# The first embedding's gate in seven block products, and all late weights in pools on one side

## The chip, the core and the metric

The kernel runs on one core of a Trainium2 chip. The metric is the device time of one execution in microseconds. Three runs of the kernel before took 3415.33, 3416.30 and 3417.81; the median is 3416.3. The engines are PE (matrix products, into PSUM), DVE (vector), ACT (scalar functions and copies), POOL (a second vector engine) and SP, which issues the DMAs. Each works through its own instructions in order, and semaphores tie them together.

## What is computed

The reference is a two-layer encoder over 2048 + 256 tokens of width 1024, in float32. What the change touches comes after the first layer's attention and after the second layer's mixer:

```python
h = h + y                                                   # y: attention's output projection
gate = jax.nn.sigmoid(rms_norm(h, norm_ple[0]) @ w_ple_gate[0])
h = h + gate * (p[0] @ w_ple_proj[0])                       # first embedding
y = mixer_c(rms_norm(h, norm_mix[1]), w_in_c, w_grp_c, scale_c, w_out_c)
h = h + y                                                   # y ends with @ w_out_c
gate = jax.nn.sigmoid(rms_norm(h, norm_ple[1]) @ w_ple_gate[1])
h = h + gate * (p[1] @ w_ple_proj[1])                       # second embedding
```

## The kernel before

Every product of two float32 matrices is made of three matmuls of the type fp32r: both operands are split in a high and a low part, and high x high, high x low and low x high are summed in PSUM (`mm3`, L176). In the trace such a triple reads `wh,ah`, `wl,ah`, `wh,al`: the first name is the operand that streams through (`wh`, `wl`: parts of the weights), the second the one that stands in the array (`ah`, `al`: parts of the activations). In the mixer the weights stand and the activations stream.

The program runs in stages: the first projections; attention A beside the second half of the projections; attention B beside "fill" work (output projection, embedding projections, folding of the mixer's weights, all by `drive`, which mixes a main generator and a fill generator by costs); the rest of the fill; then, from about 2370 us in the profile, the part that the change rewrites:

- The **gate of the first embedding** takes 18 tiles of 128 tokens. For each, `norm_rows` (L182) makes the normalised rows `xn` (ACT for the squares, POOL for the scale), `quarter` (L980) turns four blocks by PE transposes into `pt`, `part` (L973) splits them into `ah` (ACT) and `al` (DVE), and `gate_half` (L950) makes 512 columns of the product in 8 chunks of 128 channels, that is 24 matmuls, then the sigmoid (ACT), the product with the embedding `pp` and the sum with the residual `xr` (DVE). Its weights `WG0` stand in the pools `ple0a` and `ple0b`, opened from the right side of SBUF.
- In the same loop `halves_sums` (L1029) makes sums of weights for the two later stages: loads of four quarter blocks, four differences on POOL, four stores (`to_d`, `tg_d`).
- The **mixer** works on blocks of 256 tokens and four groups `g`. A group has two products of 48 matmuls x 256 columns: `pg` with `WG[g]`, `pz` with `WU[g]`. Its weights stand in four pools `wc0` to `wc3`, opened from the left side; `load_c` (L1011) fills them.
- The **mixer's output projection and the second embedding's gate** (`Pair`, L1120, and the loop at L1343) use Strassen's scheme in Winograd's form on pairs of token tiles: two by two blocks, seven products of 4 chunks x 3 = 12 matmuls instead of eight. `Pair.prepare` makes the sums of activations for the next pair, `Pair.use` adds up the products. The seven weight blocks (`BLK`) take over the mixer's pools (`HOME`); `block_w` (L1091) loads and splits one. While the last pair of the output projection runs, each block is replaced by that of the gate.

The order of instructions on each engine is set when the program is built: a scheduler places them by simulated times, within what the pools' and tiles' waits allow. Weights and stagings come through `slot()`, four buffers of 128x512 (`wst`). All loads and stores go through SP's queue.

A tile's place in SBUF is fixed in the built program. There the tiles `ah`, `al` and the gate's `wh`, `wl` (pools from the right) start 32 bytes beside a multiple of 64; the mixer's and the seven products' `wh`, `wl` (pools from the left) start at multiples of 64, as do all operands of the first projections.

Of the kernel before, what the change touches and what calls it, by code (L numbers as in the profile page):

```python
# [11 lines left out]
F32 = mybir.dt.float32  # L12
# [21 lines left out]
WG_A = 6  # L34
# [5 lines left out]
def trunk_kernel(ctx: ExitStack, tc: tile.TileContext, ins, outs):  # L40
# [37 lines left out]
    t_d = [[dscratch(f"t{n}{i}_d", [512, 512]) for i in range(4)] for n in "og"]  # L78
# [675 lines left out]

    ahead = {}
# [25 lines left out]
    def proj_out(k0):  # L781
# [22 lines left out]
        for i, tq in enumerate(todo):  # L804
# [5 lines left out]
            for a in (0, 512):  # L810
                xr, nx = nx, before(i, a + 512)
                ps = fill_ps()
                for c in range(4):
                    mm3(ps, (yh[:, c], yl[:, c]), W[a // 512][c], c == 0, c == 3)
                    if c == 1:
                        yield 1.3 * (OUTK if k0 else 1.0)
                ve.tensor_tensor(out=xr, in0=ps, in1=xr, op=ALU.add)
                sy.dma_start(h_d[tq : tq + P, a : a + 512], xr)
                if a == 0:
                    y = fetched(i + 1)  # L820
                    if k0 == 0 and i == len(todo) - 1:
                        fill_w(("ple", 0))
                yield 1.3 * (OUTK if k0 else 1.0)

# [125 lines left out]
    def gate_half(pw, layer, W, n_, tq, a, pg, sg, xr, dst):  # L950

        cols = slice(a, a + 512)
        if a == 0:
            sg.append(pw.tile([P, D], F32, tag="pp", name="pp", bufs=1))
            sy.dma_start(sg[1], pp_d[layer][tq : tq + P])
        for c in range(KC):
            mm3(pg, [x[:, c % 4] for x in n_[c // 4]], (W[c][0][:, cols], W[c][1][:, cols]), c == 0, c == KC - 1)
        ac.activation(sg[0][:, cols], pg, AF.Sigmoid)
        ve.tensor_tensor(out=sg[0][:, cols], in0=sg[1][:, cols], in1=sg[0][:, cols], op=ALU.mult)
        ve.tensor_tensor(out=xr[:, cols], in0=xr[:, cols], in1=sg[0][:, cols], op=ALU.add)  # L960
        if a:
            sy.dma_start(dst, xr)

    xr_ = [(0, NXR)]

    def loaded(tq):
        o, n = xr_[0]
        xr_[0] = (o + 1) % n, n
        xr = (late if o == NXR else work).tile([P, D], F32, tag=f"xr{o}", name="xr", bufs=1)
# [17 lines left out]
    def turned(xn):  # L987
        return [part(quarter(xn, k), ve) for k in range(2)]

    ple0 = [ExitStack(), ExitStack()]  # L990
    wpg = ins["w_ple_gate"][0]
    pw = ple0[0].enter_context(tc.tile_pool(name="ple0a", bufs=1, side="right", reuse_waits="tile"))
    WG0 = load_w(pw, wpg[: WG_A * P], WG_A * P, [(0, D)], "wg", gple[0][:, :WG_A])
    for _ in fill:
        pass
    keep.close()
    sS_.close()
    xr = loaded(0), loaded(P)
    pw = ple0[1].enter_context(tc.tile_pool(name="ple0b", bufs=1, side="right", reuse_waits="tile"))
    WG0 += load_w(pw, wpg[WG_A * P :], D - WG_A * P, [(0, D)], "wg", gple[0][:, WG_A:])  # L1000
    n_ = turned(norm_rows(work, xr[0]))

    wc = ins["w_in_c"][0]
    WU, WG = [], []
    wp = []

    def pair_w(g, c):

        return [wp[g].tile([P, 512], F32R, tag=f"{x}{c}", name=f"w{x}", bufs=1) for x in "hl"]

    def load_c(g):  # L1011

        wp.append(ctx.enter_context(tc.tile_pool(name=f"wc{g}", bufs=1, reuse_waits="tile")))
        both = [pair_w(g, c) for c in range(KC)]
        for to, src, o in ((WU, m_d, g * 256), (WG, wc, D + g * 256)):
            i = 0 if to is WU else 256
            got = [[t[:, i : i + 256] for t in b] for b in both]
            for c in range(0, KC, 2):
                st = slot().rearrange("p (k w) -> p k w", k=2)
                sy.dma_start(st, src[c * P : (c + 2) * P, o : o + 256].rearrange("(k p) w -> p k w", p=P))  # L1020
                for k in range(2):
                    split_w(st[:, k], *got[c + k], gmix[1][:, c + k : c + k + 1])
            to.append(got)

    first_x = []

    w_tail = ins["w_out_c"][0], ins["w_ple_gate"][1]

    def halves_sums(pool, n, c):  # L1029

        q = []
        for i in range(4):
            k, a = divmod(i, 2)
            b = pool.tile([P, 512], F32, tag=f"q{i}", name="q", bufs=2)
            sy.dma_start(b, w_tail[n][k * 512 + c * P : k * 512 + c * P + P, a * 512 : a * 512 + 512])
            if n:
                ac.activation(b, b, AF.Copy, scale=gple[1][:, k * 4 + c : k * 4 + c + 1])
            q.append(b)
        b11, b12, b21, b22 = q
        for i, (out, x, y) in enumerate(((b11, b12, b11), (b12, b22, b12), (b22, b22, b11), (b21, b21, b22))):  # L1040
            po.tensor_tensor(out=out, in0=x, in1=y, op=ALU.subtract)
            sy.dma_start(t_d[n][(0, 2, 1, 3)[i]][c * P : c * P + P], out)

    for tq in range(0, T, P):
        more = tq + P < T
        sg = [pw.tile([P, D], F32, tag="sg", name="sg")]
        if more:
            xn = norm_rows(work, xr[1])
        else:
            first_x.append(norm_rows(work, loaded(0)))  # L1050
        gate_half(pw, 0, WG0, n_, tq, 0, po_(), sg, xr[0], h_d[tq : tq + P])
        if more:
            n2 = turned(xn)
        else:
            first_x.append(norm_rows(work, loaded(P)))
        gate_half(pw, 0, WG0, n_, tq, 512, pf_(), sg, xr[0], h_d[tq : tq + P])
        if more:
            xr, n_ = (xr[1], loaded(tq + 2 * P) if tq + 2 * P < T else None), n2
        if tq == 4 * P:
            load_c(0)  # L1060
        if tq // P - 6 in range(8):
            halves_sums(pw, *divmod(tq // P - 6, 4))

    def turned2(xn):

        got = []
        for j in range(4):
            pt = pt_()
            for c in range(2):
                for i in range(2):  # L1070
                    pe.transpose(pt[:, (c * 2 + i) * P : (c * 2 + i + 1) * P], xn[i][:, (j * 2 + c) * P : (j * 2 + c + 1) * P], ident)
            got.append([x.rearrange("p c t -> p (c t)").rearrange("p (c t) -> p c t", t=NB) for x in part(pt, ve)])
        return got

    x0 = turned2(first_x)
    for p_ in ple0[::-1]:
        p_.close()

# [7 lines left out]
    def spare(kind):  # L1086
        tags = {"tmp": ("h4", "l4", "h5"), "g": ("l5", "h6", "l6", "h7", "l7")}[kind]
        turns[kind] += 1
        return wp[0].tile([P, 512], F32R, tag=tags[turns[kind] % len(tags)], name=kind, bufs=1).bitcast(F32)
# [18 lines left out]
    def temp():  # L1108
        return spare("tmp")
# [301 lines left out]
```

## Time and profile before

| | us |
|---|---|
| median of three runs (3415.33 to 3417.81) | 3416.3 |
| the profiled execution, in all | 3424.23 |
| its span, first to last instruction | 3422.4 |
| PE busy | 3348.8 |
| ACT / DVE / POOL busy | 1766.1 / 2123.2 / 1882.1 |

The profile is of one execution. The page gives the busy time of each engine, the chain of work that ended last, and the costliest groups of instructions. Answers of the trace give the same for single stretches: sums by stage, instructions in order of time, and who waited for whom. Ends of matmuls are modelled and overlap the next one; the time that a matmul takes in a stream is therefore read from start to start. The stages that the change rewrites lie at about 2370 to 2610 (gate), 2610 to 3032 (mixer), 3032 to 3218 (mixer's output projection) and 3218 to 3422 us (second gate).

### The profile page before, as it was taken

To read this page: it belongs to the slowest core of one execution; us is meant where nothing else is said; L and a number is where in the kernel's file an instruction comes from. 1 tells how busy PE (TensorE), PEld (TensorE's weight loads), DVE (VectorE), ACT (ScalarE), POOL (GpSimd) and SP (SyncE) were. 2 spreads that over 40 slices of the span, in tenths; PEclk is the share of its full clock that TensorE was granted. 3 is DMA by queue.
4 is the path that set the end of the run, shared out by engine and by line. 5 is a ranking of instruction groups with operands and counts; after the bars stand their busy time and mean duration, and the time that the engine had idled before them with its cause. 6 is when DMAs were issued, how large, how long until landed. Compare 5 with 4: busy or idle time off the path is not lost.

```text
span 3422.4 us, 60525 instructions
## 1 busy us (share of the span) xinstructions
PE 3348.8 (98%) x21478; PEld 2981.5 (87%) x21478; DVE 2123.2 (62%) x4461; ACT 1766.1 (52%) x3257; POOL 1882.1 (55%) x2106
## 2 busy tenths in 40 slices
PE   9999999999999999999999998999999999999999
PEld 8998999998899988888888887887788999988777
DVE  5347666677666677768879787873545222175656
ACT  5326666666666666645767776562435121132543
POOL 6775545454644455446867677881522333265665
PEclk9999999999999999999999999999999999999999
DMA  9654323234422323664444634427945111155543
GB/s 296 197 167 142 107 79 106 83 108 127 140 85 85 103 78 110 183 188 131 124 141 142 185 99 124 133 86 253 344 157 189 55 50 42 40 188 172 176 141 126
DMA packets 465766, 469.22 MB, mean 137 GB/s; under 512 B 35896, under 2 KB 388664, under 8 KB 464440
## 3 DMA queue, kind: packets, MB, share of 16 engines
q1 hardware_dynamic: 465464, 465.35, 43.9%
q8 instruction: 170, 2.79, 0.3%
q14 instruction: 132, 1.08, 0.1%
HBM read 292.21 MB, written 173.02 MB: 136 GB/s over the span
## 4 chain that ended last, share of the span: by engine, by line
PE 84%; DMA 5%; DVE 4%; issue 2%; POOL 2%; ACT 2%; SPq 0%; DVEq 0%; ACTq 0%; POOLq 0%
PE pf L178 10%; PE pf L180 10%; PE pf L179 10%; PE pt L370 9%; PE pa L408 6%; PE pa L409 6%; PE po L178 5%; PE po L180 5%; PE po L179 5%; PE po L502 3%; PE po L501 3%; PE pa L178 3%; PE pa L179 3%; PE pa L180 3%; DMA xr<-h_d 1%
## 5 line engine op out<-in xcount | busy, mean ns | idle before, releaser
L420 ACT ACTIVATE s<-s,mx 128x1024 f32<-128x1024 f32 x512 | 585.7, 1147 | 174.2 <-DVE mx L654 90.1
L378 DVE TENSOR_TENSOR pl<-pt,ph 128x512 fp32r<-128x512 f32 x780 | 523.6, 685 | 202.4 <-ACT ph L374 198.8
L374 ACT CAST ph<-pt 128x512 fp32r<-128x512 f32 x780 | 437.1, 584 | 260.6 <-PE pt L370 125.4
L370 PE MATMUL pt<-ident,s 128*128 128x128 f32 x3120 | 468.3, 273 | 6.0 <-DVE pl L378 4.5
L370 PEld LDWEIGHTS pt<-ident,s 128*128 128x128 f32 x3120 | 370.2, 141 | 56.7 <-issue 6.8
L654 DVE CUSTOM_DVE_ANT_0 s<-pa,dist,mx 128x512 f32<-128x512 f32 x384 | 286.1, 746 | 50.2 <-PE pa L409 34.9
L674 POOL TENSOR_TENSOR s<-s 128x1024 f32<-128x1024 f32 (+1 forms) x136 | 314.2, 2328 | 0.2
L483 POOL TENSOR_SCALAR s<-s,rs 128x1024 f32<-128x1024 f32 (+1 forms) x272 | 297.8, 1107 | 12.1
L473 DVE TENSOR_SCALAR_CACHE_REDUCE s<-pa,mx 128x512 f32<-128x512 f32 x384 | 285.7, 744 | 23.1 <-PE pa L409 14.0
L501 PE MATMUL po<-ph,vA 128*128 128x256 f32 x1040 | 282.8, 294 | 0.6 <-ACT ph L374 0.6
L502 PE MATMUL po<-pl,vA 128*128 128x256 f32 x1040 | 280.2, 296 | 1.1 <-DVE pl L378 1.1
L408 PE MATMUL pa<-kk,q 128*128 128x512 f32 (+1 forms) x528 | 220.8, 421 | 20.6 <-DMA q<-qTh_d 9.6
L113 POOL TENSOR_TENSOR rstd<-rstd,mhalf 128x1 f32<-128x1 f32 (+3 forms) x154 | 166.5, 1081 | 114.8 <-DVE rstd L112 101.7
L408 PE MATMUL pa<-kA,q 128*128 128x512 f32 (+1 forms) x528 | 223.1, 423 | 3.6 <-DVE s L473 3.4
L409 PE MATMUL pa<-kA,q 128*128 128x512 f32 (+1 forms) x528 | 208.6, 395 | 0.0
L409 PE MATMUL pa<-kk,q 128*128 128x512 f32 (+1 forms) x528 | 207.6, 396 | 0.2 <-DMA q<-qTl_d 0.2
L501 PEld LDWEIGHTS po<-ph,vA 128*128 128x128 f32 x1040 | 197.5, 190 | 10.3 <-ACT ph L374 1.0
L502 PEld LDWEIGHTS po<-pl,vA 128*128 128x128 f32 x1040 | 197.8, 190 | 7.0 <-DVE pl L378 3.0
L178 PE MATMUL pf<-wh,xh 128*128 128x512 f32 (+1 forms) x576 | 195.4, 339 | 0.3 <-DVE vl L596 0.3
L180 PE MATMUL pf<-wh,xl 128*128 128x512 f32 (+1 forms) x576 | 194.6, 338 | 0.0
L179 PE MATMUL pf<-wl,xh 128*128 128x512 f32 (+1 forms) x576 | 194.4, 337 | 0.0
L479 POOL TENSOR_TENSOR sm<-sm 128x1 f32<-128x1 f32 x128 | 26.2, 204 | 290.1 <-ACT s L420 289.8
(269 smaller groups left out, 10140.2 us busy)
## 6 DMA issues: line engine op xcount, KB each, us to landing
xr<-h_d SPq DMA_DIRECT2D x72, 512.0 KB, 3.3
q<-qTh_d SPq DMA_DIRECT2D x144, 128.0 KB, 3.0
q<-qTl_d SPq DMA_DIRECT2D x144, 128.0 KB, 2.9
xh<-xTh_d SPq DMA_DIRECT2D x18, 1024.0 KB, 5.4
xl<-xTl_d SPq DMA_DIRECT2D x18, 1024.0 KB, 8.4
h_d<-xr SPq DMA_DIRECT2D x72, 256.0 KB, 3.4
pp_d<-xr SPq DMA_DIRECT2D x72, 256.0 KB, 2.1
pp<-pp_d SPq DMA_DIRECT2D x36, 512.0 KB, 4.2
```

Of the source, the lines that this page charges most:

```text
L178: pe.matmul(out, lhsT=lhs[0], rhs=rhs[0], start=first, stop=False)
L179: pe.matmul(out, lhsT=lhs[0], rhs=rhs[1], start=False, stop=False)
L180: pe.matmul(out, lhsT=lhs[1], rhs=rhs[0], start=False, stop=last)
L370: pe.transpose(pt[:, (c * 2 + i) * P : (c * 2 + i + 1) * P], s[:, (c0 + c) * P : (c0 + c + 1) * P], ident)
L374: ac.copy(ph, pt)
L378: ve.tensor_tensor(out=pl, in0=pt, in1=ph.bitcast(F32), op=ALU.subtract)
L408: pe.matmul(ps, lhsT=q1, rhs=k[:, i * 512 : i * 512 + w], start=True, stop=False)
L409: pe.matmul(ps, lhsT=q2, rhs=k[:, i * 512 : i * 512 + w], start=False, stop=True)
L420: ac.activation(s[:, c], s[:, c], AF.Exp, bias=bias, scale=-1.0, accum_out=sums[i])
L501: pe.matmul(ov[0][:, 0:256], lhsT=v, rhs=ph[:, c], start=c0 + c == 0, stop=False)
L502: pe.matmul(ov[0][:, 0:256], lhsT=v, rhs=pl[:, c], start=False, stop=c0 + c == nk - 1)
L674: po.tensor_tensor(out=sc[0][:, k], in0=sc[0][:, k], in1=sc[1][:, k], op=ALU.subtract)
```

## The change

- The first embedding's gate becomes a third stage of seven block products (`n = 2`, with the weights `w_ple_gate[0]`). `gate_half`, `turned` and the pools `ple0a`, `ple0b` go. The loop over pairs becomes a function `seven`, called once for stage 2 and once for stages 0 and 1. The first pair of stage 2 is prepared, and its first two weight blocks are split, while the output projection ends; the next two blocks follow once the projection's memory is free, the last three in the first pair.
- Eight pools `w0` to `w7`, all opened from the right side, hold the weight blocks, the mixer's weights and the sums of activations in turn. `load_c` takes half a group (4 of 8 chunks); the first four halves are loaded in the last pair of stage 2, the others in the mixer's first block.
- The sums of weights go through `slot()` and are made in steps: those of stage 2 on POOL in the first 12 tiles of attention's output projection (`proj_out(0)`), those of stages 0 and 1 on DVE in the mixer, from its third block on.
- `Pair.prepare` takes the quarter `a11` before `a21`, in all stages; stage 2 stores its halves to `h_d`.
- The mixer turns its next block's rows in its second group, not ahead of the first; there are five buffers `xr` instead of four until the mixer begins.

```diff
-WG_A = 6
+    stored = []
...
                 sy.dma_start(h_d[tq : tq + P, a : a + 512], xr)
+                stored.append((k0, tq, a))
                 if a == 0:
+                    next(weight_sums, None)
                     y = fetched(i + 1)
...
+    w_seven = ins["w_out_c"][0], ins["w_ple_gate"][1], ins["w_ple_gate"][0]
+    g_seven = None, gple[1], gple[0]
+    def quarters(n, c):
+        q = []
+        for i in range(4):
+            k, a = divmod(i, 2)
+            b = slot()
+            sy.dma_start(b, w_seven[n][k * 512 + c * P : k * 512 + c * P + P, a * 512 : a * 512 + 512])
+            if n:
+                ac.activation(b, b, AF.Copy, scale=g_seven[n][:, k * 4 + c : k * 4 + c + 1])
+            q.append(b)
+        return n, c, q
+    def sums_of(n, c, q):
+        b11, b12, b21, b22 = q
+        for i, (out, x, y) in enumerate(((b11, b12, b11), (b12, b22, b12), (b22, b22, b11), (b21, b21, b22))):
+            (po if n == 2 else ve).tensor_tensor(out=out, in0=x, in1=y, op=ALU.subtract)
+            sy.dma_start(t_d[n][(0, 2, 1, 3)[i]][c * P : c * P + P], out)
+            if i == 1:
+                yield
...
-    def gate_half(pw, layer, W, n_, tq, a, pg, sg, xr, dst):
-        for c in range(KC):
-            mm3(pg, [x[:, c % 4] for x in n_[c // 4]], (W[c][0][:, cols], W[c][1][:, cols]), c == 0, c == KC - 1)
...
-    HOME = dict(zip(BLK, ((0, 0), (1, 0), (1, 4), (2, 0), (2, 4), (3, 0), (3, 4))))
+    HOME = [dict(zip(BLK + ["sums"], p)) for p in ((0, 2, 3, 4, 5, 6, 7, 1), (0, 2, 3, 4, 5, 6, 7, 1), (0, 1, 2, 3, 4, 5, 6, 7))]
+    def open_w(*pools):
+        for j in pools:
+            wp[j] = ctx.enter_context(tc.tile_pool(name=f"w{j}", bufs=1, side="right", reuse_waits="tile"))
...
+    def seven(stages, step, ends, more):
+        pairs = [Pair(n, t0) for n in stages for t0 in range(0, T, 2 * P)]
+        pairs[0] = step
+        for i, p in enumerate(pairs):
+            nx = pairs[i + 1] if i + 1 < len(pairs) else None
+            step = nx.prepare() if nx else ends()
...
+                if more:
+                    b = more.pop(0)
+                    W[p.n][b] = block_w(p.n, b)
...
+    open_w(0, 1, 7)
+    for b in BLK[:2]:
+        W[2][b] = block_w(2, b)
+    first_pair = Pair(2, 0)
+    step = first_pair.prepare()
+    next(step)
+    for _ in fill:
+        if len(stored) % 2 == 0:
+            next(step, None)
...
+    keep.close()
+    sS_.close()
+    open_w(2, 3, 4, 5, 6)
+    for b in BLK[2:4]:
+        W[2][b] = block_w(2, b)
...
+        seven([2], first_pair, to_mixer, BLK[4:])
...
+                if t0 == 0 and g < 2:
+                    load_c(2 * g + 4)
+                    load_c(2 * g + 5)
+                if t0 >= 2 * NB:
+                    next(weight_sums, None)
```

In the order of PE, at the end of attention's output projection (`whi`, `wlo`, `yh`, `yl`), the gate before stands between the projection's products as halves of 24 matmuls, alternating in `po` and `pf`:

```order
L180 MATMUL pa<-whi,yl 128x512
L180 MATMUL pf<-wh,al 128x512
L178 MATMUL pf<-wh,ah 128x512
L179 MATMUL pf<-wl,ah 128x512
L180 MATMUL pf<-wh,al 128x512
```

In the changed kernel the first pair's products stand there in blocks of 12, after the projection's last product, and PE waits for ACT, DVE and POOL, which split the weight blocks, between them; transposes of the next pair's rows lie in between:

```order
L179 MATMUL pa<-wh,al 128x512
L1007 MATMUL pt<-ident,xn 128x128 x3
L1007 MATMUL pt<-ident,xn 128x128 [waits PE_49]
L1007 MATMUL pt<-ident,xn 128x128 x3
L177 MATMUL pa<-wh,ah 128x512 [waits Activation_49]
L178 MATMUL pa<-wl,ah 128x512 [waits DVE_49]
L179 MATMUL pa<-wh,al 128x512
L177 MATMUL pa<-wh,ah 128x512 [waits Activation_49]
L178 MATMUL pa<-wl,ah 128x512 [waits Pool_49]
L179 MATMUL pa<-wh,al 128x512
```

So blocks that wait for their weights one by one now stand where halves of 24 matmuls on one tile of rows stood.

On POOL, in attention, where the output projection begins (`sm`, `rs`: sums of the softmax; `s`: its rows; `yt`, `yh`, `yl`: attention's output), before:

```order
L479 TENSOR_TENSOR sm<-sm 128x1 [waits Activation_49]
L481 TENSOR_TENSOR rs<-sm,minus 128x1 [waits Pool_49]
L483 TENSOR_SCALAR s<-s,rs 128x1024 [waits DVE_49,Pool_49]
L483 TENSOR_SCALAR s<-s,rs 128x1024 [waits DVE_49]
L515 TENSOR_TENSOR yt<-yt,gt 128x128 [waits DMAHW3_49,DVE_49]
L122 TENSOR_SCALAR yh<-yt 128x128 [waits DMAHW7_49,Pool_49]
L123 TENSOR_TENSOR yl<-yt,yh 128x128 [waits DMAHW2_49,Pool_49]
```

and in the changed kernel, with the sums of weights (`st<-st`) between the softmax's steps:

```order
L478 TENSOR_TENSOR sm<-sm 128x1 [waits Activation_49]
L847 TENSOR_TENSOR st<-st 128x512 [waits DMAHW3_49,DVE_49,Activation_49]
L480 TENSOR_TENSOR rs<-sm,minus 128x1 [waits Pool_49]
L514 TENSOR_TENSOR yt<-yt,gt 128x128 [waits DVE_49]
L482 TENSOR_SCALAR s<-s,rs 128x1024 [waits PE_49,Pool_49]
L482 TENSOR_SCALAR s<-s,rs 128x1024
L121 TENSOR_SCALAR yh<-yt 128x128 [waits DMAHW7_49,Pool_49]
L122 TENSOR_TENSOR yl<-yt,yh 128x128 [waits DMAHW2_49,Pool_49]
L847 TENSOR_TENSOR st<-st 128x512 [waits DMAHW4_49,Activation_49]
L847 TENSOR_TENSOR st<-st 128x512 [waits DMAHW6_49,Pool_49]
```

A sum waits for a load and for ACT's scaling, and the next scaling of softmax rows stands behind it.

## Rows read from the trace of the kernel before

**Rows 1.** The page: busy time by engine; chain that ended last, by engine.

```profile
PE 3348.8 (98%) x21478; PEld 2981.5 (87%) x21478; DVE 2123.2 (62%) x4461; ACT 1766.1 (52%) x3257; POOL 1882.1 (55%) x2106
...
PE 84%; DMA 5%; DVE 4%; issue 2%; POOL 2%; ACT 2%; SPq 0%; DVEq 0%; ACTq 0%; POOLq 0%
```

**Rows 2.** Stages: window, length, PE PEld DVE ACT POOL busy (count), clock, DMA share, GB/s.

```profile
1360.00:1550.00 190.00, 186.48 (x1104) 162.21 (x1103) 134.38 (x313) 103.04 (x193) 86.91 (x121) 0.99 0.64 190
...
2290.00:2370.00 80.00, 75.14 (x395) 63.05 (x394) 34.71 (x61) 23.96 (x42) 23.17 (x27) 0.96 0.71 225
...
2412.00:2610.00 198.00, 197.09 (x930) 163.92 (x929) 86.93 (x115) 67.47 (x124) 70.88 (x77) 1.00 0.65 227
2610.00:3032.00 422.00, 418.30 (x3565) 417.26 (x3564) 135.43 (x298) 110.16 (x211) 151.17 (x198) 1.00 0.24 76
3032.00:3218.00 186.00, 186.00 (x823) 150.84 (x822) 120.86 (x169) 63.84 (x110) 110.84 (x82) 1.00 0.57 185
3218.00:3422.00 204.00, 189.05 (x862) 151.25 (x861) 125.26 (x167) 84.58 (x152) 126.25 (x118) 0.99 0.44 139
```

**Rows 3.** PE in order of time, gate: start, length, instruction, tiles, count.

```profile
2574.36 0.39 PE L178 MATMUL po<-wh,ah 128*128 128x512 f32 x1
...
2579.80 1.03 PE L984 MATMUL pt<-ident,xn 128*128 128x128 f32 x8
2580.59 0.48 PE L178 MATMUL pf<-wh,ah 128*128 128x512 f32 x1
```

**Rows 4.** PE in order of time, mixer's output projection: first rows, 48 matmuls apart.

```profile
3098.99 0.40 PE L178 MATMUL pa<-wh,ah 128*128 128x512 f32 x1
...
3110.19 0.40 PE L178 MATMUL pf<-wh,ah 128*128 128x512 f32 x1
```

**Rows 5.** PE in order of time, mixer: 48 matmuls apart.

```profile
2984.18 0.28 PE L178 MATMUL pf<-ah,wh 128*128 128x256 f32 x1
...
2989.78 0.28 PE L178 MATMUL po<-ah,wh 128*128 128x256 f32 x1
```

**Rows 6.** PE in order of time, first projection: starts of runs.

```profile
113.50 0.39 PE L178 MATMUL pa<-wh,xh 128*128 128x512 f32 x1
...
117.58 0.28 PE L178 MATMUL po<-xh,wh 128*128 128x256 f32 x1
...
117.93 0.28 PE L178 MATMUL po<-xh,wh 128*128 128x256 f32 x1
...
121.89 0.28 PE L178 MATMUL po<-xh,wh 128*128 128x256 f32 x1
```

**Rows 7.** Waits of PE, 2290 to 2420: us in total, times, longest.

```profile
PE pa L178 <- DVE xr L817: 4.0, 1, 4.0
PE po L178 <- ACT sg L958: 1.7, 1, 1.7
```

**Rows 8.** Waits of PE, 3000 to 3422.

```profile
PE pt L984 <- POOL xn L187: 5.3, 6, 2.7
PE pt L984 <- ACT tmp L1145: 1.0, 1, 1.0
PE pf L179 <- POOL wl L1100: 0.8, 1, 0.8
```

**Rows 9.** Groups, whole run: count, busy us, mean ns, idle time before and its releasers.

```profile
L1041 POOL TENSOR_TENSOR q<-q 128x512 f32<-128x512 f32 x32 | 43.7, 1365 | 45.3 <-DMA q<-in_w_out_c_dram 41.1 <-ACT q L1037 2.0 <-POOL q L1041 0.6
L1100 POOL TENSOR_TENSOR wl<-st,wh 128x512 fp32r<-128x512 f32 x16 | 23.5, 1476 | 15.9 <-ACT wh L1099 15.9
L1099 ACT CAST wh<-st 128x512 fp32r<-128x512 f32 x32 | 19.3, 620 | 14.6 <-DMA st<-tg_d 9.5 <-DMA st<-to_d 4.8
L1100 DVE TENSOR_TENSOR wl<-st,wh 128x512 fp32r<-128x512 f32 x16 | 15.4, 964 | 10.6 <-ACT wh L1099 10.6
```

**Rows 10.** Waits of PE, 2420 to 2700.

```profile
PE po L178 <- ACT sg L1291: 3.4, 2, 3.0
```

**Rows 11.** Waits of PE, whole run.

```profile
PE pa L408 <- DMA q<-qTh_d: 9.6, 2, 7.2
```

More of the change, by code (lines that the diff above doesn't have):

```diff
@@ L823, in proj_out, with all_sums @@
                 yield 1.3 * (OUTK if k0 else 1.0)
+    w_seven = ins["w_out_c"][0], ins["w_ple_gate"][1], ins["w_ple_gate"][0]
[17 more added lines that the diff above has]
+                yield
+    def all_sums(stages):
+        for n in stages:
+            for c in range(4):
+                q = quarters(n, c)
+                yield
+                yield from sums_of(*q)
+                yield
+    weight_sums = all_sums([2])
     def proj_ple(layer):
@@ L948, in trunk_kernel @@
     work = ctx.enter_context(tc.tile_pool(name="work", bufs=2, side="right", reuse_waits="tile"))
[L950 to L964 removed]
+    xr_, late = [(0, NXR + 1)], []
     def loaded(tq):
@@ L985, in quarter @@
         return pt
[L987 to L1062, printed above, removed]
@@ new lines, in turned2, with to_mixer @@
+    def turned2(xn, got):
+        for j in range(4):
+            pt = pt_()
+            for c in range(2):
+                for i in range(2):
+                    pe.transpose(pt[:, (c * 2 + i) * P : (c * 2 + i + 1) * P], xn[i][:, (j * 2 + c) * P : (j * 2 + c + 1) * P], ident)
+            got.append([x.rearrange("p c t -> p (c t)").rearrange("p (c t) -> p c t", t=NB) for x in part(pt, ve)])
+            if j == 1:
+                yield
+    x0 = []
+    def to_mixer():
+        xn = [norm_rows(work, loaded(t)) for t in (0, P)]
+        yield
+        yield
+        load_c(0)
+        load_c(1)
+        turn = turned2(xn, x0)
+        next(turn)
+        yield
+        next(turn, None)
+        load_c(2)
+        yield
+        load_c(3)
+        yield
@@ L1260, in trunk_kernel @@
         sc_ = pc.tile([P, 4, 2, 8], F32, name="sc_")
-        def chain(t0):
-            return turned2([norm_rows(work, loaded(t0 + tt * P)) for tt in range(2)])
         ZW = NB + 24
@@ L1271, in trunk_kernel @@
             if t0 + NB < T:
-                nxt = chain(t0 + NB)
+                xn = [norm_rows(work, loaded(t0 + NB + tt * P)) for tt in range(2)]
             for g in range(4):
                 w = WINDOWS[g]
+                if g == 1 and t0 + NB < T:
+                    nxt = []
+                    for _ in turned2(xn, nxt):
+                        pass
                 pg, pz = po_(), pf_()
```

132 lines of the change are left out of this document (68 added, 64 removed).

## Prediction

> **What bounds the kernel now.** I read the page first, to see which engine fills the span: PE is busy for 98% of it, and the chain that ended last is PE for 84% [rows 1]. A gain must therefore come out of PE's own stream, and other engines matter only where PE waits for them. Next I read the busy time by stage [rows 2], to see where PE has holes: the first embedding's gate (2412 to 2610) has 0.9 us of idle time in 198, the mixer 3.7 in 422, the output projection of the mixer none in 186, the second embedding's gate 15 in 204, and the seam between attention and the first gate (2290 to 2370) 4.9 in 80. The granted clock is 1.00 in all of them but the seam (0.96) and the last stage (0.99), so PE works at the 2.4 GHz level. In three of the stages time is the number of matmuls times the pace from one start to the next. That pace I read from the timeline, over runs without a wait:
>
> - gate now, 512 columns: 24 matmuls from 2574.36 to 2579.80, 226.7 ns each; the 8 transposes behind them take 0.79 [rows 3];
> - seven products, 512 columns: 48 from 3098.99 to 3110.19, 233.3 ns each [rows 4];
> - mixer, 256 columns: 48 from 2984.18 to 2989.78, 116.7 ns each [rows 5];
> - first projection: 33 of 256 columns from 117.93 to 121.89, 120.0 ns each, and 18 of 512 columns from 113.50 to 117.58, 226.7 ns each [rows 6].
>
> The last line matters because it shows that neither 226.7 nor 120.0 belongs to one stage's form of loop. What sets apart the two stages that deviate (233.3 where others have 226.7, 116.7 where others have 120.0) is, in the built program, where the two operands stand: there the weights lie in pools opened from the left, which start at multiples of 64 bytes, and the activation parts in `work`, opened from the right, 32 bytes beside such a multiple. In the gate both are 32 beside, in the first projection both on a multiple. That the pace follows from this is my inference from four stages, not something that a row states.
>
> **The change part by part.** *Fewer products.* The gate has 18 tiles x 2 halves x 8 chunks x 3 = 864 matmuls; seven products over 9 pairs need 9 x 7 x 4 x 3 = 756. 108 matmuls x 226.7 ns [rows 3] = 24.5 us less, all on PE and so on the path. Transposes stay at 144.
>
> *Pace of the stages whose weights move.* The weights of all three seven-product stages and of the mixer now lie in pools opened from the right. In the built program of the changed kernel every one of these matmuls has both operands 32 beside a multiple of 64. If the pace follows, the two old seven-product stages go from 233.3 to 226.7: 1512 matmuls x 6.6 = 10.0 us less. The mixer goes from 116.7 to 120.0: 9 x 4 x 96 = 3456 matmuls x 3.3 = 11.4 us more. The two nearly cancel. The bounds for each are nothing (the pace stays with the loop) and these values; I take the values, since the gate, with both operands so placed, ran at 226.7 for its whole stage [rows 3].
>
> The Trainium skill (TensorE: Matmul & The Clock Gate, section Back-to-back issue gap) gives the gap of a warm stream as columns / 2.4 + 2.5 ns, 215.7 ns for 512, with no term for where an operand lies. The rows are 11 to 18 ns above it at the same granted clock. By the page the 108 matmuls would be worth 23.3 us and the move of the weights nothing; that outcome is the first rival below.
>
> *Seam from attention to the gate.* Before, PE idled 4.0 there for DVE's evacuations and 1.7 for a sigmoid [rows 7]. Two of the seven weight blocks are split under the tail of the output projection; the other five, 20 tiles, wait for memory that the projection frees, and are split in the first pair. A tile costs 0.62 on ACT and 0.96 on DVE or 1.48 on POOL [rows 9]: 12.4 us of ACT, 12 x 0.96 = 11.5 of DVE, 8 x 1.48 = 11.8 of POOL, beside a pair's own work. In the second gate's stage that is POOL 126/9 = 14.0, DVE 13.9, ACT 9.4 us a pair [rows 2]. So POOL and DVE need some 25 us in a pair in which PE has 84 x 0.2267 + 1.6 = 20.6. PE's order puts the second pair's first blocks between, which covers most of the 5 us. The same exchange of seven blocks between the two old stages cost PE 1.0 + 0.8 [rows 8], with the pools already free. I take 3 us over the seam of before; bounds -5 (today's holes vanish) and +12 (the blocks arrive one by one).
>
> *The new gate's steady pairs.* The old second gate lost 5.3 us in six waits for a normalised row [rows 8]; the new order takes the quarter of the first row tile first, whose row is normalised earlier. I take 2 us for the new stage (0 to 5) and 2 less for the old one (0 to 5 less).
>
> *Seam to the mixer.* Before, eight chunks of the first group's weights had long been split; now they go into the blocks that the last pair has used, 16 casts of 256 columns before the first group can end. The wait of 3.0 for a SiLU behind such casts [rows 10] stays, and I add 2 (0 to 6).
>
> *Sums of weights.* The 32 old sums leave POOL in the gate (1.37 us each [rows 9]), where it had 127 us to spare [rows 2]: nothing gained. In the mixer they run on DVE, busy for 135 us of 422, and its 64 DMAs meet a DMA share of 0.24 [rows 2]: nothing lost, covered by some 287 us of DVE; without that cover 32 x 0.96 = 31 us. The 16 new ones run on POOL between the softmax steps of attention: 16 x 1.37 = 21.9 us where POOL has 87 of 190 busy [rows 2]. I take 0; bounds -5 and +8, because every later instruction of attention's second half is also reordered, and its largest waits (7.2 for a block of queries [rows 11]) may move either way. Behind a sum that waits for its load stand the scaling of the next softmax on POOL and, on SP, the loads of queries behind the sum's store.
>
> **Sum:** -24.5 - 10.0 + 11.4 + 3 + 2 - 2 + 2 = -18.1 us. The profiled execution has a span of 3422.4 and 3424.2 in all, 8 above the median of 3416.3; I take the difference from the median: 3398 us.
>
> **The rivals.** *The pace belongs to the loop, not to the place.* Then the new stage runs like the old seven-product stages, 756 x 233.3 = 176.4 against 864 x 226.7 = 195.9, 19.5 less, the mixer stays, and with the same +5 for seams and pairs it is -14.5: 3402. For it: both old stages of that loop have 233.3 throughout. Against it: the first projection's 512-column runs, also a loop with fresh stationary operands for each matmul.
>
> *Only the long matmuls gain.* 512 columns go to 226.7 and the mixer keeps 116.7: -24.5 - 10.0 + 5 = -29.5, 3387. For it: runs of 256 columns with both operands 32 beside a multiple are short in this trace. Against: the first projection's long ones are at 120.0.
>
> *The first pair is bound by its weights.* If each of the five blocks is waited for, the 25 us of POOL and DVE stand on the path with their loads: some 15 us more than summed, 3413. For it: two DVE and two POOL splits a block. Against: the second pair's blocks fill in.
>
> *Slower than before.* Attention's POOL chain becomes the path: each of 16 sums costs its 1.37 and the waits of its scaled load, some 2 us, in a place where PE's next transposes need the scaled softmax: 16 x 2 = 33 us, -18 + 33 = +15, 3431. It decides once POOL has no slack between two softmax halves; against it stands that POOL is under half busy there [rows 2].
>
> **How the numbers follow.** Forecast 3398, with its own range of 3391 to 3408: 0.50; loop's pace 3402: 0.17; mixer keeps its pace 3387: 0.15; weights bind 3413: 0.11; slower 3431: 0.07. The range 3383 to 3412 leaves out the last case and half of the fourth, and the far ends of the seams. A measurement of this kernel can tell about 0.2%, 7 us, from no change; so faster means below 3409.5: 0.50 + 0.16 + 0.15 + 0.02 = 0.83; the same 0.10; slower 0.07.
>
> **What would show it.** In the changed profile 756 matmuls of 512 columns in the first gate; pace 226.7 in all three seven-product stages and 120.0 in the mixer (over 48 matmuls 5.76 us instead of 5.60); idle time of PE below 15 us from the attention's end to the second pair; no wait of PE for the sums in attention. Wrong it would be if the mixer stays at 116.7, if PE waits for weight blocks pair after pair, or if attention's second half becomes longer by more than 8 us.

## The result, and the profile after

The change makes the kernel slower: median 3459.8 us of four runs (3454.6 to 3464.5) against 3417.1 of four runs before, ratio 1.0123 (95% interval 1.0106 to 1.0139). Forecast were 3398 us and a range of 3383 to 3412, so the sign was wrong too. The profiled execution of after took 3454.6, span 3452.8, against 3422.4 before [rows 1]: 30.4 us more. The medians lie 42.7 apart, so the stages below, read from the two profiled executions, show some 12 us less than the medians do.

The page of after, busy time of TensorE (PE) and shares of the chain that ended last:

```profile
PE 3350.8 (97%) x21370; PEld 2982.9 (86%) x21370; DVE 2170.0 (63%) x4551; ACT 1809.5 (52%) x3330; POOL 1976.2 (57%) x2170
...
PE 73%; DMA 8%; DVE 6%; POOL 5%; issue 4%; ACT 2%; SPq 0%; DVEq 0%; ACTq 0%; POOLq 0%
```

PE has 108 instructions fewer and yet is as long busy as in [rows 1], and its share of the chain fell from 84% to 73%: other engines now stand in it. Where, the stages show. Windows of after (start and end, length, busy time and count of PE, PEld, DVE, ACT, POOL, granted clock, DMA share, GB/s): end of attention A, attention B, seam, gate, mixer, the two last stages.

```profile
1368.00:1498.00 130.00, 124.13 (x715) 107.61 (x716) 82.78 (x187) 72.61 (x129) 66.09 (x87) 0.97 0.78 237
1498.00:2316.00 818.00, 783.10 (x4778) 675.27 (x4778) 645.24 (x1558) 533.32 (x1006) 593.33 (x588) 0.98 0.44 131
2316.00:2404.00 88.00, 84.06 (x440) 70.51 (x439) 38.00 (x65) 27.48 (x50) 31.82 (x38) 0.96 0.75 249
2404.00:2629.00 225.00, 211.40 (x967) 171.41 (x965) 139.85 (x195) 101.57 (x189) 136.26 (x124) 0.97 0.53 170
2629.00:3070.00 441.00, 435.57 (x3586) 434.43 (x3587) 156.76 (x334) 119.27 (x221) 155.10 (x201) 0.99 0.34 112
3070.00:3448.00 378.00, 365.20 (x1656) 297.00 (x1654) 235.71 (x323) 146.59 (x257) 240.92 (x199) 0.99 0.50 162
```

The same two stretches of attention in the kernel before, from the start of the output projection to the last score of half A, and half B to its last score:

```profile
1366.00:1474.00 108.00, 108.00 (x675) 95.53 (x674) 79.78 (x185) 65.60 (x118) 46.82 (x71) 1.00 0.59 173
1474.00:2291.00 817.00, 788.50 (x4824) 680.66 (x4822) 652.83 (x1562) 531.10 (x1004) 591.42 (x589) 0.99 0.46 136
```

Attention took 925 and takes 948: it has lost 23 us, where the forecast had none. Half A now holds 40 instructions of PE more and half B 46 fewer; work has moved from one half to the other. The seam (2291 to 2371 before) takes 88 instead of 80. The gate (2371 to 2610 before, 2404 to 2629 now) has become 14 us shorter instead of 24.5, with 13.6 us of idle time in 225 instead of 3.2 in 239. The mixer is 16 longer, of which the forecast pace explains 11.4; the end is 7 shorter, where the pace alone would give 10. PE of after in order of time (start, length), 48 matmuls apart: mixer, then the mixer's output projection.

```profile
2909.05 0.28 PE L178 MATMUL po<-al,wh 128*128 128x256 f32 x1
...
2914.82 0.28 PE L178 MATMUL pf<-al,wh 128*128 128x256 f32 x1
...
3142.11 0.39 PE L178 MATMUL po<-wl,ah 128*128 128x512 f32 x1
...
3152.99 0.39 PE L178 MATMUL pa<-wl,ah 128*128 128x512 f32 x1
```

5.77 us / 48 = 120.2 ns where [rows 5] had 116.7, and 10.88 / 48 = 226.7 where [rows 4] had 233.3: both as forecast.

These paces hold at the full clock, and the granted clock fell too: its mean over the span is 0.988, before it was 0.994. In the gate it is 0.97, where it was 1.00. PE of after in the gate, in order of time, and two windows (the clock is the third number from the end):

```profile
2464.70 0.39 PE L179 MATMUL pf<-wh,al 128*128 128x512 f32 x1
2468.25 1.97 PE L1007 MATMUL pt<-ident,xn 128*128 128x128 f32 x8 [3.16 <-POOL xn L186]
2469.87 0.78 PE L177 MATMUL po<-wh,ah 128*128 128x512 f32 x1
2470.44 0.63 PE L178 MATMUL po<-wl,ah 128*128 128x512 f32 x1
2470.87 0.63 PE L179 MATMUL po<-wh,al 128*128 128x512 f32 x1
```

```profile
2461.00:2464.00 3.00, 3.00 (x15) 2.48 (x14) 0.00 (x0) 0.72 (x1) 0.00 (x0) 1.00 0.50 162
2470.00:2473.00 3.00, 3.00 (x9) 2.33 (x8) 3.00 (x5) 0.04 (x1) 0.67 (x1) 0.50 0.79 259
```

PE waited 3.16 us for a normalised row. Behind the wait the clock is 0.50, the 1.2 GHz level: two matmuls of 512 columns start 0.43 us apart instead of 0.23, and the eight transposes take 1.62 us instead of 0.79 [rows 3]. So a wait can cost more than its own row says. By the means and spans, (1 - 0.988) x 3452.8 is 41 us of full clock that PE did not get, against 21 before. These 20 us more are an estimate and an upper bound, since PE was not at work in all of that time.

### The profile page after: what moved, and what is told of

It reads as the page before. It is cut to its first block, busy times and chain, and to the rows that moved or that the text cites. A ratio compares the mean times of both kernels' runs of the same rounds, so it can differ in the third digit from the quotient of the medians.

```text
span 3452.8 us, 60712 instructions
## 1 busy us (share of the span) xinstructions
PE 3350.8 (97%) x21370; PEld 2982.9 (86%) x21370; DVE 2170.0 (63%) x4551; ACT 1809.5 (52%) x3330; POOL 1976.2 (57%) x2170
## 4 chain that ended last, share of the span: by engine, by line
PE 73%; DMA 8%; DVE 6%; POOL 5%; issue 4%; ACT 2%; SPq 0%; DVEq 0%; ACTq 0%; POOLq 0%
PE pt L369 9%; PE pf L177 8%; PE pf L178 8%; PE pf L179 8%; PE pa L407 6%; PE pa L408 5%; PE po L177 4%; PE po L178 4%; PE po L179 4%; PE po L501 3%; PE po L500 3%; PE pa L177 3%; PE pa L178 3%; PE pa L179 3%; POOL al L1000 1%
```

## Experiments

Times differ by some us from chip to chip (the kernel before had medians of 3412 to 3419 beside the runs below), so what is compared are ratios to the kernel before on the same chip. 0.001 is 3.4 us. In the quoted expectations TensorE, VectorE, ScalarE, GpSimd and SyncE are PE, DVE, ACT, POOL and SP.

### Are the sums in attention the loss?

**No sums.**

```diff
-                    next(weight_sums, None)
                     y = fetched(i + 1)
...
-                sy.dma_start(st, t_d[n][int(b[1])][c * P : c * P + P])
+                src = w_seven[n][c * P : c * P + P, :512] if n == 2 else t_d[n][int(b[1])][c * P : c * P + P]
+                sy.dma_start(st, src)
```

> The changed kernel without the 16 sums of weights in attention. Part of the computation is left out: the four summed blocks of the first gate are loaded from plain quarters of the weight matrix instead, so that every later load, cast and product keeps its number and size. Theory (the sums stretch attention): the stretch from the start of the output projection to the first transposes of the gate's stage, 24 us of lost PE time longer in the changed kernel, returns to that of the kernel before; the whole is 3432 to 3440 us, ratio to the kernel before 1.004 to 1.007, and PE has no idle time between 1366 and 1474. Rival (the loss in attention comes from the freer order of instructions or from the state of the chip, not from the sums): the whole stays above 3448.

Measured 1.0015 (1.0005 to 1.0025). The sums cost 1.0123 - 1.0015, some 37 us, more than the 24 read from the profile. Without them the change is 5 us slower than before, not 18 faster.

**Scaling one step later.** The four loads of a chunk and their scaling stand in two steps instead of one.

> The changed kernel with the same 16 sums, but the scaling of a weight quarter on ScalarE stands one step of the output projection behind the issue of its load (before: directly behind it). Theory (ScalarE stands in order and waits for the loads, and the softmax and the casts of the probabilities stand behind it): ScalarE's idle time ahead of the 16 scalings falls from some 30 us to under 5, and 10 to 20 us of the 24 come back: 3440 to 3450 us. Rival (the sums' own time on GpSimd, 16 x 1.29 us, or their stores in SyncE's queue ahead of the loads of queries): within 6 us of the changed kernel, 3454 to 3464.

Measured 1.0119 (1.0106 to 1.0132): nothing gained, but the edit had not done what it was for. From 1366 to 1460 ACT's scalings waited for their loads 17.1 us in 5 waits in after, and 19.6 in 7 waits in this run. The scheduler that orders the program put loads and scalings together again. The run tells nothing of the theory.

**No scaling; transfers only; work only.** Three kernels that take the sum apart.

```diff
-            if n:
+            if n == 1:                      # no scaling for the first gate
                 ac.activation(b, b, AF.Copy, scale=...)
...
-            (po if n == 2 else ve).tensor_tensor(...)
+            if n < 2:                       # transfers only: no subtraction either
+                ve.tensor_tensor(...)
...
+            if n == 2 and c:                # work only: chunk 0's quarters again, no load
+                b = first_q[i]
```

> The changed kernel with its 16 sums in attention, their loads and their stores, but without ScalarE's scaling of the weight quarters by the norm's gain (this part of the computation is left out). Three things come with a sum: ScalarE waits for its load, GpSimd works 1.29 us and waits in its place, and 8 MB more go through the DMA engines in 85 us. Theory A (ScalarE's wait in order is the cause): most of the 35 us that the sums cost come back, ratio to the kernel before 1.002 to 1.005. Theory B (GpSimd, which now waits for the loads itself): ratio stays at 1.010 to 1.013. Theory C (the transfers): the same, 1.010 to 1.013.

> The changed kernel with the loads and stores of the 16 sums in attention, but neither ScalarE's scaling nor GpSimd's subtraction (left out: what is stored is the plain quarter). Theory A (ScalarE) and theory B (GpSimd) both expect the kernel without sums: ratio 1.001 to 1.004. Theory C (8 MB more beside attention's own loads, DMA share 0.87 instead of 0.50 in that stretch, and SyncE's queue): 1.009 or more.

> The changed kernel with all 16 scalings on ScalarE and all 16 subtractions on GpSimd at their place, but the quarters are loaded once, for the first chunk, and worked on again for the other three, and only the last chunk's results are stored (the rest of the sums is left out). Theory (it is the waits in order for the loads, 17 us on ScalarE and what follows on GpSimd, not the work itself): ratio to the kernel before 1.001 to 1.005, as without sums or little above. Rival (12 us of ScalarE and 21 us of GpSimd in 85 us are the cost): 1.009 to 1.013.

Measured: no scaling 1.0055 (1.0042 to 1.0069), transfers only 1.0018 (1.0009 to 1.0027), work only 1.0088 (1.0071 to 1.0104). The 8 MB are free (theory C falls): with transfers only, PE idles 1.7 us from 1366 to 1460, at a DMA share of 0.88 (1.5 and 0.64 without sums). Without scaling 14 us are left over the kernel without sums, and they stand where the sums stand. Waits of PE from 1367 to 1488 without scaling, and in after from 1368 to 1500:

```profile
PE pt L369 <- POOL s L482: 8.5, 2, 5.1
```

```profile
PE po L500 <- ACT ph L373: 5.3, 2, 3.2
```

POOL's scaled softmax, or ACT's cast of the probabilities, stands behind a sum that waits for its load, and PE's transposes or products wait for that. (Without scaling, POOL's subtractions waited 22.6 us for loads, in 4 waits; in after ACT's scalings waited 17.1.) But "work only" has no such wait (in 1371 to 1492 PE waits 0.7 us, for a row of `yh`), and yet it costs 25 us over the kernel without sums. The theory that it is the waits explains the smaller part; the rival (the work itself) doesn't fit either, since in that kernel no time is lost where the work is done. What after, "scaling later" and "work only" share is the order of PE's instructions: counted in the built programs, 228 matmuls of the output projection stand ahead of the last score of half A and 372 ahead of the 48th score matmul of half B in after, "scaling later" and "work only"; 167 and 300 in the kernel before, and without sums, without scaling, and with transfers only.

**The order alone.** No sums, but twelve small copies that nothing waits for.

```diff
+                    nidle[0] += 1
+                    if nidle[0] <= 12:
+                        idle = slot()
+                        ac.activation(idle[:, :P], ones, AF.Copy, scale=2.0)
                     y = fetched(i + 1)
```

> The kernel without sums in attention (four summed blocks loaded from plain quarters, as before), with twelve small copies of 128x128 on ScalarE instead, one in each of twelve steps of the output projection, which read a constant and which nothing waits for. They move the order of TensorE's instructions as the sums do: at the last score of attention's first half 228 matmuls of the output projection stand ahead instead of 167, at the 48th of the second half 372 instead of 300. Theory (the order costs the 20 us in attention's second half): that half loses some 20 us between 1780 and 2000, ratio to the kernel before 1.006 to 1.009. Rival (it is the work of the sums): ratio 1.001 to 1.003, as without sums.

Measured 1.0079 (1.0066 to 1.0093): 22 us from twelve copies of a constant. Windows 1780 to 2000 without sums, and with the copies; then PE's largest wait for the softmax there without, and its waits with:

```profile
1780.00:2000.00 220.00, 214.06 (x1392) 188.13 (x1392) 188.68 (x433) 160.18 (x305) 167.53 (x161) 1.00 0.51 153
```

```profile
1780.00:2000.00 220.00, 200.12 (x1253) 173.57 (x1252) 177.89 (x394) 148.25 (x281) 156.60 (x148) 0.96 0.47 140
```

```profile
PE pa L407 <- DVE mx L653: 1.8, 4, 0.7
```

```profile
PE pa L407 <- DVE mx L653: 8.1, 7, 4.7
PE pt L369 <- DVE pl L377: 4.9, 4, 1.9
PE pa L407 <- issue: 2.9, 1, 2.9
PE pf L177 <- ACT xr L891: 2.5, 1, 2.5
```

In the same 220 us PE starts 139 fewer instructions. It is idle for 19.9 us instead of 5.9, and the granted clock is 0.96 instead of 1.00: 14 us, and some 9 more of full clock (0.04 x 220), which together are about the 22. The two largest waits, 13.0 us, are for the softmax of half B, some 400 us behind the copies: the trace has all twelve from 1369.9 to 1375.7, 0.3 us each. "Work only" has the same four rows in that window to within 0.2 us. Each copy takes one of the four staging buffers, but that is not what costs: "transfers only" takes them 16 times in the old order and loses some 1 us over the kernel without sums. So the cost of the new order (of all engines; the counts above are PE's) is shown: some 22 us. That the fill work which the order has pulled ahead is what covered these waits is my reading of it.

**Another place for the sums.** Twice the whole computation: in the steps of the embedding's projection, and spread over the second projection beside half A.

> The changed kernel with the whole computation, but the 16 sums stand some 250 us later, in the steps of the embedding's projection, and the scaling of a quarter stands one step behind the issue of its load. Theory (the loss is due to where the sums stand: the end of attention's first half, where the second half's keys, values and the projection's weights are loaded too): DMA share there stays under 0.6, ScalarE waits less than 5 us for the loads, and the whole is within 8 us of the kernel without sums: ratio to the kernel before 1.002 to 1.004. Rival (16 sums cost some 35 us wherever they stand in attention): 1.010 or more.

> The whole computation of the changed kernel, its 16 sums moved into attention's first half, one piece at each of 32 steps of the second projection: the loads two steps ahead of the scalings, each subtraction in a step of its own. Theory (a sum costs nothing where its loads have landed and no other step of the softmax stands close behind it): ScalarE and GpSimd wait under 2 us for the loads, and the whole is that of the kernel without sums, ratio 1.000 to 1.004. Rival (every one of the 32 pieces pushes a step of the softmax on which PE waits): 1.006 or more.

Measured 1.0073 (1.0059 to 1.0086) and 1.0049 (1.0036 to 1.0062). Neither reached the kernel without sums, though the second left half B alone (811.5 us from the last score of half A to its own last, 810.7 without sums). The first has the old order at both counts (167 and 300) and lost its 20 us in half B, where its sums stand: 830.7 us there, and ACT waited 11.1 us for their loads. Written in 32 steps of half A, the second's sums were scheduled into 318 to 387, the loads right ahead of the scalings again (ACT waits 8.8 us for them in 7 waits). PE's waits from 281 to 1366 that a run without sums has not, or has smaller (there 0.6 for `ph`):

```profile
PE po L555 <- ACT ph L373: 4.8, 3, 2.8
PE pf L177 <- ACT gs L634: 4.3, 2, 3.4
```

So 20 and 12 us of the 37 are left; both results lie between theory and rival.

### What do the ends of the gate cost?

**The gate without five of its blocks; without the mixer's first weights too.** Both on the kernel without sums.

```diff
+        if n == 2 and b not in BLK[:2]:     # both
+            return W[2][BLK[0]]
...
+        if j < 4:                           # second only: no loads of groups 0 and 1
+            for to, i in ((WG, 256), (WU, 0)):
+                to[g][k * 4 : k * 4 + 4] = [[x[:, i : i + 256] for x in y] for y in kept]
+            return
```

> The kernel without sums in attention, and in the first gate five of the seven weight blocks are not loaded and cast: their products take the first block's tiles (this part of the computation is left out). The gate's stage has 26 us of stalls there, against 10 in the kernel before with the same paces: some 13 in the first two pairs, 10 at the seam to the mixer. Theory (the first two pairs are bound by the casts of the five blocks, and the wait for GpSimd's normalised row follows from its casts): 8 to 13 us less in the first two pairs, nothing changes at the seam to the mixer; ratio to the kernel before 0.997 to 0.9995. Rival (the first pairs wait for the normalised rows whatever the casts do): under 4 us.

> The kernel without sums in attention and without the weights' loads and casts at both ends of the gate: five of its seven blocks and the mixer's first two groups take the tiles of the gate's first block (left out, with the results that hang on them). Theory (the gate's and the mixer's loss of some 25 us beside their paces is the weight blocks that arrive one by one at both ends): gate and mixer together 20 to 28 us shorter than without sums alone, ratio to the kernel before 0.993 to 0.996. Rival (the rows' normalisation, the SiLU and the casts of parts take the place): under 8 us, ratio 0.999 to 1.002.

Measured 1.0009 (1.0000 to 1.0018) and 0.9979 (0.9970 to 0.9988). PE's waits in the first two pairs, 2380 to 2450, without sums:

```profile
PE pt L1006 <- POOL xn L186: 2.9, 1, 2.9
PE pa L177 <- ACT wh L130: 1.2, 1, 1.2
```

Without the five blocks the trace lists no wait of PE in that stretch, the one for the normalised row included: it followed from the casts on POOL. But the time came back at the next seam: from the last score of half B to the gate's end 295 us instead of 308, then to the mixer's end 456 instead of 441. The theory that nothing changes there failed. PE's largest waits from 2560 to 2720 without sums, without the five blocks, and without both ends' weights:

```profile
PE po L177 <- ACT sg L1321: 5.4, 3, 2.8
PE po L177 <- ACT wh L130: 3.4, 1, 3.4
PE pt L1244 <- DVE al L999: 2.8, 1, 2.8
```

```profile
PE po L177 <- ACT sg L1323: 10.2, 4, 4.5
PE po L179 <- DVE wl L131: 2.8, 4, 1.0
```

```profile
PE po L177 <- ACT sg L1328: 5.4, 2, 4.3
```

With no weights at either end 12 us are gone, between the theory's 20 to 28 and the rival's 8. So the weight blocks that arrive while PE already needs them are a good part of what gate and mixer lose, not all. What the rest is, no run here shows.

### What sets the pace of a matmul?

**32 bytes.** The kernel before with one more constant.

```diff
+    pad = const.tile([P, 8], F32, name="pad")
+    ve.memset(pad, 0.0)
```

> The kernel before, with one more constant of 32 bytes per partition, which moves every pool opened from the left by 32 bytes; no other instruction changes. Theory (the pace of matmuls follows from the two operands' start addresses modulo 64 bytes): mixer from 116.7 to 120.0 ns per 256-column matmul (+11.4 us over 3456), both seven-product stages from 233.3 to 226.7 ns per 512-column matmul (-10.0 us over 1512), in the whole within 4 us of the kernel before. Rival (the pace belongs to the loop or to the pool's side): paces stay 116.7 and 233.3.

Measured 1.0025 (1.0015 to 1.0036), 8.5 us, where 1.4 were expected; the paces moved exactly as expected (48 matmuls of the mixer in 5.76 us, 48 of 512 columns in 10.88). The other 7 us I can't assign.

**Pace without the loss in the mixer.** The kernel before, its parts laid so that the seven-product stages have equal places and the mixer unequal ones.

> The kernel before, with the cast activation parts laid so that in the seven-product stages they start at the same place modulo 64 bytes as the weights, and in the mixer 32 bytes beside them; the first gate stays as it is. Theory: 226.7 in the seven-product stages and 116.7 still in the mixer, -10.0 us: 3406 to 3410 us, ratio 0.997. Rival (the pace is a matter of the loop): no change, 3413 to 3420.

Measured 1.0054 (1.0041 to 1.0067): slower, and my rule fell. The parts lay 4128 bytes apart there, so that they agreed with the weights modulo 64 but not modulo 256. Paces account for some 7 of the 18 us that it lost (an estimate from the trace's means: 118 to 119 ns in the mixer, 231 in the first gate and in the seven-product stages); the rest is not assigned. PE in order of time, first rows of four products of 12 matmuls:

```profile
3102.40 0.39 PE L178 MATMUL pf<-wh,a 128*128 128x512 f32 x1
...
3105.13 0.40 PE L178 MATMUL pa<-wh,a 128*128 128x512 f32 x1
...
3107.92 0.39 PE L178 MATMUL po<-wh,a 128*128 128x512 f32 x1
...
3110.72 0.39 PE L178 MATMUL pf<-wh,a 128*128 128x512 f32 x1
```

Distance is here the start of the streaming operand (the weights) less that of the standing one (the part), modulo 256, worked out from the built program. It is 0 for the first product, 128 for the second and 192 for the third: 227.5, 232.5 and 233.3 ns a matmul. Over the whole stage the means of the parts were 227 to 229 at distance 0, 229 to 230 at 64, 232 to 233 at 128 and 233 at 192.

**The rule modulo 256, twice.** All parts in one tile at one place modulo 256; first handed out in turn, then in the order in which the products release them.

```diff
-        hi, lo = (work.tile([P, 512], F32R, tag=f"a{x}", name=f"a{x}", bufs=8) for x in "hl")
+        k = free.pop(0)
+        o = k * 1024 + other * 8            # other: 0 gate, 1 seven products, 2 mixer
+        hi, lo = parts[:, o : o + 512], parts[:, o + 512 : o + 1024]
```

> The kernel before, its cast activation parts in one tile and so that every part starts at the same place modulo 256 bytes: in the first gate and the seven-product stages at that of the weights, in the mixer 32 bytes behind that of the weights, as it is now. Theory (the pace of matmuls follows from the distance of the operands' starts modulo 256 bytes, since parts at 64, 128 and 192 bytes from it had 229 to 233 ns): 226.7 ns in the seven-product stages, 116.7 in the mixer; -10.0 us, ratio 0.996 to 0.998, unless the one tile adds waits. Rival (what made the parts of the earlier try slow is something else than their place): no pace changes, or both lie between, ratio 1.000 to 1.005.

> The kernel before with the same places modulo 256 bytes as in the last try (226.7 ns in the seven-product stages, 116.7 in the mixer), and the eight parts of the one tile handed out in the order in which products release them. Theory (the last try lost its 10 us again to a wait of some 1.3 us in each pair, because it handed the parts out in a fixed turn): the waits of the last two stages return to those of the kernel before, ratio 0.996 to 0.998. Rival (the waits belong to the one tile): 1.001 to 1.004.

Measured 1.0022 (1.0013 to 1.0030) and 0.9956 (0.9944 to 0.9969). In both the paces are those of the theory; the second, in order of time, 48 matmuls apart:

```profile
2921.35 0.28 PE L178 MATMUL po<-a,wh 128*128 128x256 f32 x1
...
2926.95 0.28 PE L178 MATMUL pf<-a,wh 128*128 128x256 f32 x1
...
3114.91 0.39 PE L178 MATMUL pa<-wh,a 128*128 128x512 f32 x1
...
3125.79 0.39 PE L178 MATMUL pf<-wh,a 128*128 128x512 f32 x1
```

116.7 and 226.7 ns in one kernel. The first of the two lost it again by one wait in each pair, PE's largest in the last two stages:

```profile
PE po L178 <- DVE xr L1188: 7.3, 6, 1.6
```

In the second that wait is 0.3 us in all. It is 15 us faster than the kernel before, the fastest of all kernels here. 10 of the 15 are the pace; where the other 5 come from is not shown.

**Both together.** The changed kernel with its sums spread and the mixer's parts 32 bytes behind the weights.

> The whole computation of the changed kernel, with its sums spread over attention's first half and the mixer's parts laid 32 bytes behind the weights modulo 256, handed out in the order of their release. Theory: 11 us less than with the spread sums alone, in the mixer, ratio 1.000 to 1.003, so still not below the kernel before, since 10 us of the sums and 20 of the gate's ends stay. Rival (the losses add up otherwise, since the planner moves the rest): outside 0.998 to 1.004.

Measured 1.0022 (1.0013 to 1.0031), 9 us below the spread sums alone, as expected: with two of its losses mended the change is still not below the kernel before.

## Why the prediction was wrong

- **Fewer products, -24.5: right.** Where the gate runs undisturbed its 226.7 ns hold, and PE's idle time (10 us more) and the clock of 0.97 behind its waits separate 225 us from the expected 215.
- **Paces, -10.0 and +11.4: right in size, wrong in the reason's measure.** The four runs on it show that the place of the operands decides, but modulo 256 bytes, not 64. (The padded kernel as a whole still lost 8.5 us, not 1.4.) The rivals "the pace belongs to the loop" and "only the long matmuls gain" fall with after's rows alone. The gap of 215.7 ns that the Trainium skill gives for back-to-back matmuls (TensorE: Matmul & The Clock Gate, section Wait — 56ns, not 53.3ns?; the section that the prediction names has the formula for an isolated matmul) was reached by none of these streams, the best had 226.7.
- **Sums in attention, 0 with bounds -5 and +8: this step failed.** They cost some 37 us. I argued from POOL's 87 busy us in 190 [rows 2], but an engine with half its time free still holds up what is queued behind a wait: about 14 us are that. It is the mechanism of the rival that I gave 0.07, at 3431, only on ACT as well as on POOL. The larger part, 22 us, I had named and not priced: "every later instruction of attention's second half is also reordered". I bounded it by the largest wait there, 7.2 us [rows 11]; it was many small ones in another place, with a lower clock behind them. My sign for it, half B longer by more than 8 us, did not show (818 against 817 us), because half A had taken some of its work.
- **Seam, first pair, steady pairs and seam to the mixer, 3 + 2 + 2: too small.** From the kernel without sums, 5 = -24.5 - 10.0 + 11.4 - 2 + x gives x = 30 instead of 7. Against the padded kernel, on the same chip and with the same paces, the stretch from the last score of half B to the mixer's end takes 749 us (308 and 441) instead of 750: of 24.5 us fewer products 1 is left, so 23 of the 30 stand there. 12 of them are the weight blocks at both ends; the other 11 are open. I had the demand right (25 us of POOL and DVE in a pair of 20.6) and then let PE's order cover most of it. The SiLU behind casts [rows 10] went from 3.4 to 5.4 us, my +2; PE's waits for the mixer's first casts and the last parts, 6.2, I had not named. The other 7 of the 30 are as much as the padded kernel loses beyond its paces, without any of the change's new order; that they are the same 7 is not shown.
- **Old second gate, 2 less: not there.** PE waits 6.2 us for normalised rows in the two last stages of after, in 8 waits, against 5.3 in 6 [rows 8].
- **The clock: no term at all.** Waits were priced at their own length. The estimate of up to 20 us above lies inside the losses named here; it is not a further one.
- **The range.** It left out the end where two mis-sized terms add up, because the only slower case stood alone, with 33 us for the sums and the seams as forecast.

## What to carry to other kernels

Where a scheduler orders the whole program, small work put into a tightly interleaved stretch has two prices: its own waits, and a new order for everything behind it. The second can't be bounded by a wait of the old trace; compare the two orders (how far the covering work has moved against the work that it covers), and if they differ, widen the range by the idle time that the old order covered. A wait costs its length and, where the clock falls behind it, the slower matmuls that follow. And work written far apart need not run apart: look where the scheduler put it before believing in a prefetch.

## What the hardware showed

In the stages compared here (first gate, mixer, seven products) the pace of a stream of fp32r matmuls depends on the distance of the two operands' starts in SBUF modulo 256 bytes, streaming less standing. With 512 columns it is 226.7 ns at distance 0 where all products have it (after, padded kernel, both kernels of the rule modulo 256). It rises over 229 to 230 (64), 232 to 233 (128) and 233 (192) (the kernel whose parts lie 4128 bytes apart) to 233.3 in the kernel before, where the standing activations lie 32 bytes behind the weights (224). With 256 columns it is 120.0 at distance 0 (after, padded kernel) and 116.7 where the streaming activations lie 32 bytes behind the weights (kernel before, both kernels of the rule). In the padded kernel's seven products the starts lie 256 bytes apart modulo 512 in the built program, and the pace is the 226.7 that the gate before has with equal starts; a rule modulo 512 would not allow that. The granted clock is 1.00 in all of these rows. A constant of 32 bytes switched both stages at once.

At the other level of the clock, granted 0.50 behind a wait of 3.16 us in after, matmuls of 512 columns start 0.43 us apart.
